# Issuing the spills of decays and convolution results from ScalarE, with two buffers for the decays and one for the results, in a hybrid attention and DeltaNet encoder

## The chip, the cores and the metric

The kernel runs on one core of one Trainium2 chip. The metric is device time in microseconds (us). Before the change three runs gave a median of 2249.93 us (2245.04 to 2252.57).

## The reference, cut to what matters

The program is an encoder of two layers, run on a prompt of 1024 tokens and a sample of 256, 1280 columns in all. Layer 0 is a neighbourhood attention, layer 1 a bidirectional gated DeltaNet with 8 heads, each with keys of 128 and values of 256. The change lies in layer 1:

```python
def _gated_deltanet(h, w_in, conv_w, a_log, dt_bias, norm_w, w_out):
    b, t, _ = h.shape
    proj = h @ w_in
...
    qkv = jax.nn.silu(_centred_depthwise_conv(proj[..., :o1], conv_w))
    z = proj[..., o1:o2].reshape(b, t, GDN_HEADS, GDN_DV)
...
    o_fwd = _chunk_gated_delta(q, k, v, g[:, :, 0], beta[:, :, 0])
    o_bwd = _chunk_gated_delta(fl(q), fl(k), fl(v), fl(g[:, :, 1]), fl(beta[:, :, 1]))
    o = (o_fwd + fl(o_bwd)).astype(h.dtype)
    o = _rmsnorm(o, norm_w) * jax.nn.silu(z)
    return o.reshape(b, t, GDN_VW) @ w_out
```

and in _chunk_gated_delta, for chunks of 64 tokens:

```python
    diff = g[..., :, None] - g[..., None, :]
    decay = jnp.where(tril, jnp.exp(jnp.where(tril, diff, 0.0)), 0.0)
    k_beta = k * beta[..., None]
    a_kk = jnp.where(tril_strict, jnp.einsum('bhncd,bhnsd->bhncs', k_beta, k) * decay, 0.0)
    lhs = jnp.eye(c, dtype=jnp.float32) + a_kk
    w = lax.linalg.triangular_solve(lhs, k_beta * jnp.exp(g)[..., None], left_side=True,
                                    lower=True, unit_diagonal=True)
```

What follows the solve is a scan over the chunks, forward and backward.

## The kernel before

The stages stand one after the other: attention (to about 640 us), its output projection and the norm (to 780), the DeltaNet's projections (gdn_proj, about 780 to 1600), the scan (to about 2040) and the output projection. All five edits lie in gdn_proj, or in what it calls.

**What TensorE does there.** For each head four blocks of 128 output channels are projected (q, k and two of v), then two gate blocks (z). A block takes three passes, wh with xh, wh with xl and wl with xh, for each of 8 slices of the inputs, over column blocks of 512, 512 and 256 (L1250). So TensorE has a stream of matmuls without end, and all else is meant to run beside it. load_w (L1191) brings a block's weights: SyncE loads wraw, ScalarE copies it to wh (L1202) and its negative to wl (L1206), and then a DMA issued by GpSimd adds the weights to wl in flight (L1207), which leaves the rounding error of wh. There are three buffers for wh and wl and one for wraw.

**What runs beside it.** Class Side (L1211) holds chains, Python generators that are stepped by the columns which the matmuls have taken: a chain that yields n is stepped again n times its pace later. The chains are:

- conv (L504): ScalarE makes the middle tap (L509), VectorE the other four (L512), and after a pause ScalarE the Silu into th (L518), which two DMAs spill to DRAM (L519 and L520).
- decays (L614), for one head: six calls of decay (L602). Each is a matmul into a PSUM bank "t" (L605, three buffers), two or four sums on VectorE from it (L608, which end the bank's use), and an exponential in place on ScalarE (L611). E holds two of these and is spilled (L624), and GpSimd adds its halves into B (L625).
- invert (L629), for one head, once its keys have left conv: k by k matmuls, four diagonal blocks turned, and then a sweep of 30 steps on VectorE (L671 and L673) that inverts 32 x 32 blocks. Two transposes (L677 and L678) end the sweep, ScalarE and GpSimd place the results (L686, L687, L692 to L694). Then decays of the next head are put on the side, and after a pause come four groups of small matmuls, L703, L710, L723 and L731, each with copies between them (L706 by ScalarE to Z behind L703; L712 to L718 behind L710; L726 by ScalarE to Z behind L723).
- the gates' z (L554 and L563 with their spills).

**What sets the order.** The program gives the Tile framework the instructions in the order in which these generators run; the framework's scheduler then sets each engine's own order by its model of when each becomes ready. So a changed yield moves what is offered when, and the engine's order follows only as far as the scheduler takes it up. Each engine runs its row in order, a DMA issue too: what stands behind a waiting issue waits with it.

Of the kernel before, what the change touches and what calls it, by code (L numbers as in the profile page):

```python
# [8 lines left out]
F32 = mybir.dt.float32  # L9
# [6 lines left out]
NP, NS = 1024, 256  # L16
T = NP + NS
# [6 lines left out]
def pool(tc, name, bufs, side="left"):  # L24
    return tc.tile_pool(name=name, bufs=bufs, side=side, reuse_waits="tile")
# [436 lines left out]
def gdn_proj(tc, a, pmm, XH, XL):  # L462

    nc = tc.nc
    with ExitStack() as st:
        ap = st.enter_context(pool(tc, "gp", 2, "right"))
        pp = st.enter_context(banks(tc, "gpi", 2, "right"))
        side = a["side"] = Side()
        Bs = {}
# [34 lines left out]
        def conv(f, r):  # L504

            h, ch = divmod(f, 4)
            m = T + 2
            acc = ap.tile([128, T + 2], F32, name="acc")
            nc.scalar.activation(acc, r[:, 2:2 + m], AF.Copy, scale=cw[:, f, 2:3])  # L509
            yield 8000  # L510
            for i in (0, 1, 3, 4):
                tap = nc.vector.scalar_tensor_tensor(acc, r[:, i:i + m], cw[:, f, i:i + 1], acc,  # L512
                                                     op0=OP.mult, op1=OP.add)
                if i == 0:
                    tc.keep_in_program_order(tap)
            yield 14000 if ch == 1 else 20000
            th = ap.tile([128, T + 2], F32, name="th")
            tc.keep_in_program_order(nc.scalar.activation(th, acc, AF.Silu))  # L518
            nc.sync.dma_start(a["qkv_dram"][f, :, :NP], th[:, :NP])  # L519
            nc.sync.dma_start(a["qkv_dram"][f, :, NP:], th[:, NP + 2:])  # L520
            if ch == 1:
                side.add(invert(tc, a, ap, pp, h, th, D, W, WT, Z, Bs), 4000, 0.85 if h == 7 else 0.95)

# [2 lines left out]
        for h, ch in order:  # L526
            f = 4 * h + ch
# [3 lines left out]
            for b in sorted(range(3), key=lambda b: (f, b) not in a["begun"]):  # L531
                t0, n = BLK[b]
# [68 lines left out]

def decay(nc, a, ap, pool, h, d, c0, n, E, nt=2):  # L602

# [3 lines left out]
    for c in range(n):  # L607
        nc.vector.scalar_tensor_tensor(E[:, c], pg[:, 128 * c:128 * c + 128],  # L608
                                       a["lbG"][:, 8 * d + h, c0 + c:c0 + c + 1], a["mask"][:, d],
                                       op0=OP.add, op1=OP.add)  # L610
    nc.scalar.activation(E, E, AF.Exp)  # L611


def decays(tc, a, ap, pp, h, Bs):  # L614

    nc = tc.nc
    B = ap.tile([128, NB, 128], F32, name="B", bufs=2)
    for c0 in range(0, NB, 4):
        n = min(4, NB - c0)
        E = ap.tile([128, 2, 4, 128], F32, name="E", bufs=1)[:, :, :n]  # L620
        for d in range(2):
            decay(nc, a, ap, pp, h, d, c0, n, E[:, d], 3)
            yield 3500
        nc.sync.dma_start(a["e_dram"][h, :, :, c0:c0 + n], E)  # L624
        nc.gpsimd.tensor_add(B[:, c0:c0 + n], E[:, 0], E[:, 1])  # L625
    Bs[h] = B


def invert(tc, a, ap, pp, h, kT, D, W, WT, Z, Bs):  # L629


    nc = tc.nc
# [3 lines left out]
    for c0 in range(0, NB, 4):  # L636
        n = min(4, NB - c0)
# [21 lines left out]
    side, quad = (a["blocks"][:, i, None, :].to_broadcast([128, NB, 128]) for i in range(2))  # L659
# [7 lines left out]
    for c in range(30, 0, -1):  # L667
        tmp = ap.tile([128, 240], F32, name="tmp", bufs=1)
        n = 31 - c
# [24 lines left out]
        nc.gpsimd.tensor_copy(W[sl[i], 1, :, q], diag(i, lo))  # L694
        yield 0
    if h < 7:
        a["side"].add(decays(tc, a, ap, pp, h + 1, Bs), 4000)
    else:
        factors(tc, a)
    yield 34000  # L700
    zt = pp.tile([128, NB, 32], F32, name="m", bufs=2)
    for c in range(NB):
        nc.tensor.matmul(zt[:, c], B32[:, c], M[:, c], start=True, stop=True)  # L703
# [44 lines left out]
def gates(tc, a, ap, pmm, pp, XH, XL):  # L748

    nc = tc.nc  # L750
# [5 lines left out]
    for b in (0, 2, 1):  # L756
        t0, n = BLK[b]
# [39 lines left out]
    eT = consts.tile([128, 16, NB], F32, name="eT")  # L797
    eTG = consts.tile([128, 16, NB], F32, name="eTG")
    pG = pp.tile([128, 16, NB], F32, name="t", bufs=3)
    tri = ap.tile([128, 2, 4, 128], F32, name="E", bufs=1)[:, :, 0]  # L800
    for d, keep in enumerate((OP.is_ge, OP.is_le)):
        nc.vector.tensor_scalar(tri[:, d], a["jp"], 0.0, None, op0=keep)
    for d in range(2):
# [700 lines left out]
```

## Time and profile before

| | us |
|---|---|
| median of three runs | 2249.93 (2245.04 to 2252.57) |
| the profiled execution's own time | 2251.55 |
| its span | 2249.7 |
| TensorE busy, share of the span | 2166.0 (96%) |
| VectorE, ScalarE, GpSimd busy | 1509.2, 1146.6, 585.1 |
| TensorE's clock, mean | 0.98 of full |

All rows of a profile come from the one profiled execution, whose time is 1.6 us over the median. A row of the instructions in order of time has its start, its length, engine, line, operation, out<-in, and in brackets the idle time of the engine ahead of it, with what ended that. Matmuls overlap, so their starts count and not their lengths. A row of waits has the engine and line that waited, on whom, and the total, the times and the longest. A row of stretches has the stretch, and for each engine its busy time in it, and behind them the clock granted to TensorE, the DMA engines' share and GB/s.

### The profile page before, as it was taken

To read this page: it belongs to the slowest core of one execution; us is meant where nothing else is said; L and a number is where in the kernel's file an instruction comes from. 1 tells how busy PE (TensorE), PEld (TensorE's weight loads), DVE (VectorE), ACT (ScalarE), POOL (GpSimd) and SP (SyncE) were. 2 spreads that over 40 slices of the span, in tenths; PEclk is the share of its full clock that TensorE was granted. 3 is DMA by queue.
4 is the path that set the end of the run, shared out by engine and by line. 5 is a ranking of instruction groups with operands and counts; after the bars stand their busy time and mean duration, and the time that the engine had idled before them with its cause. 6 is when DMAs were issued, how large, how long until landed. Compare 5 with 4: busy or idle time off the path is not lost.

```text
span 2249.7 us, 34012 instructions
## 1 busy us (share of the span) xinstructions
PE 2166.0 (96%) x12502; PEld 1881.3 (84%) x12502; DVE 1509.2 (67%) x3370; ACT 1146.6 (51%) x2313; POOL 585.1 (26%) x631
## 2 busy tenths in 40 slices
PE   8999999999999999899999999999899999999998
PEld 7789989989878877788888888888788888877887
DVE  5577777776773858768577676867566666675444
ACT  6455545555673454454544546354456666654333
POOL 2100100110230422233132313231176766600000
PEclk9999999999999999899999999999899999999999
DMA  5424342533556343443534444442675566567322
GB/s 181 112 74 118 82 118 75 125 93 97 151 150 182 98 114 89 141 127 101 159 105 134 111 136 115 128 145 71 209 207 164 168 186 180 154 216 234 107 96 85
DMA packets 148456, 300.10 MB, mean 133 GB/s; under 512 B 44976, under 2 KB 67632, under 8 KB 147264
## 3 DMA queue, kind: packets, MB, share of 16 engines
q1 hardware_dynamic: 126784, 232.89, 32.7%
q0 software_dynamic: 12096, 44.05, 11.2%
q10 hardware_dynamic: 9408, 20.98, 3.0%
q8 instruction: 99, 1.62, 0.3%
q14 instruction: 69, 0.57, 0.1%
HBM read 211.92 MB, written 75.45 MB: 128 GB/s over the span
## 4 chain that ended last, share of the span: by engine, by line
PE 70%; DVE 17%; ACT 5%; DMA 4%; issue 3%; POOL 1%; SPq 0%; ACTq 0%; DVEq 0%; POOLq 0%
PE mm L1250 42%; PE mm L1266 4%; DVE tmp L671 3%; DVE X L673 3%; PE k L1014 3%; PE o L986 2%; PE k L1005 2%; PE O L263 2%; PE o L1027 2%; PE u L986 2%; DVE acc L512 2%; PE pt L243 2%; DMA yt<-y_spill 1%; PE t L940 1%; PE S L286 1%
## 5 line engine op out<-in xcount | busy, mean ns | idle before, releaser
L1250 PE MATMUL mm<-xh,wh 128*128 128x512 f32 (+1 forms) x1920 | 700.6, 365 | 6.3 <-DVE z L554 3.2
L1250 PE MATMUL mm<-xh,wl 128*128 128x512 f32 (+1 forms) x1920 | 700.7, 365 | 3.4 <-DMA wl<-w_o 2.2
L1250 PE MATMUL mm<-xl,wh 128*128 128x512 f32 (+1 forms) x1920 | 701.9, 366 | 0.3 <-DVE xl L352 0.2
L1250 PEld LDWEIGHTS mm<-xh,wh 128*128 128x128 f32 x1920 | 367.6, 191 | 52.8 <-DVE z L554 3.8
L1250 PEld LDWEIGHTS mm<-xh,wl 128*128 128x128 f32 x1920 | 367.5, 191 | 47.6 <-DMA wl<-w_o 2.6
L1250 PEld LDWEIGHTS mm<-xl,wh 128*128 128x128 f32 x1920 | 367.7, 191 | 43.1 <-DVE xl L352 0.4
L512 DVE SCALAR_TENSOR_TENSOR acc<-raw,cw,acc 128x1282 f32<-128x1282 f32 x128 | 199.1, 1555 | 4.7 <-ACT acc L509 2.3
L1202 ACT ACTIVATE wh<-wraw 128x1024 fp32r<-128x1024 f32 x92 | 96.8, 1055 | 139.2 <-PE mm L1250 112.7
L1200 POOL CAST wh<-wraw 128x1024 fp32r<-128x1024 f32 x32 | 34.2, 1070 | 498.2 <-PE mm L1250 441.4
L1250 PE MATMUL mm<-yh,wh 128*128 128x512 f32 (+1 forms) x384 | 137.5, 359 | 2.4 <-ACT yh L1124 2.2
L1250 PE MATMUL mm<-yh,wl 128*128 128x512 f32 (+1 forms) x384 | 137.0, 358 | 1.2 <-DVE wl L1204 1.2
L1250 PE MATMUL mm<-yl,wh 128*128 128x512 f32 (+1 forms) x384 | 137.6, 360 | 0.1
L1018 DVE TENSOR_TENSOR vl<-k,vh 128x256 fp32r<-128x256 f32 x160 | 67.1, 424 | 69.6 <-ACT vh L1017 65.1
L247 ACT ACTIVATE ph<-pt 128x512 fp32r<-128x512 f32 (+2 forms) x144 | 67.6, 479 | 77.0 <-PE pt L243 65.3
L539 ACT ACTIVATE raw<-mm 128x512 f32<-128x512 f32 (+1 forms) x96 | 49.9, 522 | 101.9 <-PE mm L1250 96.1
L248 DVE TENSOR_TENSOR pl<-pt,ph 128x512 fp32r<-128x512 f32 (+2 forms) x144 | 75.2, 538 | 38.2 <-ACT ph L247 36.7
L608 DVE SCALAR_TENSOR_TENSOR E<-t,lbG,mask 128x128 f32<-128x128 f32 x160 | 46.9, 342 | 79.7 <-DMA e_spill<-E 78.8
L1206 ACT ACTIVATE wl<-wraw 128x1024 fp32r<-128x1024 f32 x84 | 88.5, 1053 | 16.3 <-DMA wraw<-w_qk 8.4
L221 ACT ACTIVATE P<-P,mx 128x384 f32<-128x384 f32 (+1 forms) x128 | 75.0, 587 | 39.6 <-DVE mx L220 38.3
L1266 PE MATMUL mm<-wh,xl 128*128 128x256 f32 x320 | 91.9, 287 | 0.6 <-POOL xl L65 0.6
L1017 ACT ACTIVATE vh<-k 128x256 fp32r<-128x256 f32 x160 | 60.6, 380 | 62.5 <-PE k L1014 59.3
L1266 PE MATMUL mm<-wl,xh 128*128 128x256 f32 x320 | 91.6, 286 | 0.5 <-DVE wl L1204 0.5
(314 smaller groups left out, 4917.1 us busy)
## 6 DMA issues: line engine op xcount, KB each, us to landing
wraw<-w_qkv SPq DMA_DIRECT2D x32, 512.0 KB, 3.7
qkv_spill<-th SPq DMA_DIRECT2D x32, 512.0 KB, 2.7
wraw<-w_go SPq DMA_DIRECT2D x32, 512.0 KB, 3.6
wl<-w_qkv POOLq DMA_DIRECT2D x30, 512.0 KB, 8.0
Al<-e_spill SPq DMA_DIRECT2D x8, 1280.0 KB, 6.7
qe<-eg_spill SPq DMA_DIRECT2D x16, 640.0 KB, 8.0
wraw<-w_qk SPq DMA_DIRECT2D x16, 512.0 KB, 3.9
wl<-w_qk POOLq DMA_DIRECT2D x16, 512.0 KB, 8.6
```

The source lines that it names most:

```text
L221: nc.scalar.activation(Pv, Pv, AF.Exp, scale=-1.0, bias=mx[:, 0:1], accum_out=mx[:, 1:2])
L247: nc.scalar.activation(view(ph), view(pt), AF.Copy)
L248: nc.vector.tensor_sub(view(pl), view(pt), view(ph))
L512: tap = nc.vector.scalar_tensor_tensor(acc, r[:, i:i + m], cw[:, f, i:i + 1], acc, op0=OP.mult, op1=OP.add)
L671: nc.vector.tensor_mul(tv, N[:, 0:c, c:c + 1].to_broadcast([128, c, n]), X[:, c:c + 1, c + 1:32].to_broadcast([128, c, n]))
L673: nc.vector.tensor_add(X[:, 0:c, c + 1:32], X[:, 0:c, c + 1:32], tv)
L986: self.tc.nc.tensor.matmul(ps, w[x], v[y], start=(first and i == 0), stop=(i == 2))
L1014: nc.tensor.matmul(pw, W[:, d, cs[d]], Y[d], start=True, stop=True)
L1202: nc.scalar.activation(wh, raw, AF.Copy)
L1206: nc.scalar.activation(wl, raw, AF.Copy, scale=-1.0)
L1250: nc.tensor.matmul(ps, w[:, k, :], x[k][b], start=(k == 0 and i == 0), stop=(k == KD - 1 and i == 2))
L1266: nc.tensor.matmul(ps, x[k][b][:, cc], w[:, k % 4, :], start=(k == 0 and i == 0), stop=(k == KD - 1 and i == 2))
```

## The change

The two DMAs that spill th are issued by ScalarE instead of SyncE, and th has one buffer instead of two. The DMA that spills E is issued by ScalarE as well, and E has two buffers instead of one. The decays of the next head are put on the side with a delay of 12000 columns instead of 4000, and each pause in them is 1.3 times as long. In the first and the last head the pause ahead of L703 is 44000 columns instead of 34000. In gates the tile tri takes the new number of buffers of E, whose name it shares.

```diff
@@ -514,10 +514,10 @@
                 if i == 0:
                     tc.keep_in_program_order(tap)
             yield 14000 if ch == 1 else 20000
-            th = ap.tile([128, T + 2], F32, name="th")
+            th = ap.tile([128, T + 2], F32, name="th", bufs=1)
             tc.keep_in_program_order(nc.scalar.activation(th, acc, AF.Silu))
-            nc.sync.dma_start(a["qkv_dram"][f, :, :NP], th[:, :NP])
-            nc.sync.dma_start(a["qkv_dram"][f, :, NP:], th[:, NP + 2:])
+            nc.scalar.dma_start(a["qkv_dram"][f, :, :NP], th[:, :NP])
+            nc.scalar.dma_start(a["qkv_dram"][f, :, NP:], th[:, NP + 2:])
             if ch == 1:
                 side.add(invert(tc, a, ap, pp, h, th, D, W, WT, Z, Bs), 4000, 0.85 if h == 7 else 0.95)
 
@@ -617,11 +617,11 @@
     B = ap.tile([128, NB, 128], F32, name="B", bufs=2)
     for c0 in range(0, NB, 4):
         n = min(4, NB - c0)
-        E = ap.tile([128, 2, 4, 128], F32, name="E", bufs=1)[:, :, :n]
+        E = ap.tile([128, 2, 4, 128], F32, name="E", bufs=2)[:, :, :n]
         for d in range(2):
             decay(nc, a, ap, pp, h, d, c0, n, E[:, d], 3)
             yield 3500
-        nc.sync.dma_start(a["e_dram"][h, :, :, c0:c0 + n], E)
+        nc.scalar.dma_start(a["e_dram"][h, :, :, c0:c0 + n], E)
         nc.gpsimd.tensor_add(B[:, c0:c0 + n], E[:, 0], E[:, 1])
     Bs[h] = B
 
@@ -694,10 +694,10 @@
         nc.gpsimd.tensor_copy(W[sl[i], 1, :, q], diag(i, lo))
         yield 0
     if h < 7:
-        a["side"].add(decays(tc, a, ap, pp, h + 1, Bs), 4000)
+        a["side"].add(decays(tc, a, ap, pp, h + 1, Bs), 12000, 1.3)
     else:
         factors(tc, a)
-    yield 34000
+    yield 44000 if h in (0, 7) else 34000
     zt = pp.tile([128, NB, 32], F32, name="m", bufs=2)
     for c in range(NB):
         nc.tensor.matmul(zt[:, c], B32[:, c], M[:, c], start=True, stop=True)
@@ -797,7 +797,7 @@
     eT = consts.tile([128, 16, NB], F32, name="eT")
     eTG = consts.tile([128, 16, NB], F32, name="eTG")
     pG = pp.tile([128, 16, NB], F32, name="t", bufs=3)
-    tri = ap.tile([128, 2, 4, 128], F32, name="E", bufs=1)[:, :, 0]
+    tri = ap.tile([128, 2, 4, 128], F32, name="E", bufs=2)[:, :, 0]
     for d, keep in enumerate((OP.is_ge, OP.is_le)):
         nc.vector.tensor_scalar(tri[:, d], a["jp"], 0.0, None, op0=keep)
     for d in range(2):
```

Nothing is computed differently, and each engine has the same instructions but for the 88 DMA issues (32 of L519, 32 of L520, 24 of L624) that ScalarE has and SyncE has no more, and one pair of table loads fewer on ScalarE. What moves is the order.

The first place is on TensorE in one of the middle heads, around the fourth of a head's six decay matmuls (t_12052 before, t_12090 after). mm_12015 is the third column block of one of the head's projections (mm_11999 after), mm_12071 and mm_12047 are the first block of the next. Before:

```order
L1250 MATMUL mm_12015<-xh6_2_7755,wl_11904 128x256
L1250 MATMUL mm_12015<-xh7_2_7758,wh_11903 128x256
L605 MATMUL t_12052<-GR_8791,one_hot_64 128x512 [waits DVE_49,PE_49]
L1250 MATMUL mm_12015<-xl7_2_7782,wh_11903 128x256
L1250 MATMUL mm_12015<-xh7_2_7758,wl_11904 128x256
L1250 MATMUL mm_12071<-xh0_0_7735,wh_12066 128x512 [waits Activation_49]
```

After:

```order
L1250 MATMUL mm_12047<-xh6_0_7753,wh_12042 128x512
L1250 MATMUL mm_12047<-xl6_0_7777,wh_12042 128x512
L1250 MATMUL mm_12047<-xh6_0_7753,wl_12043 128x512
L605 MATMUL t_12090<-GR_8791,one_hot_64 128x512 [waits DVE_49,PE_49]
L1250 MATMUL mm_12047<-xh7_0_7756,wh_12042 128x512
L1250 MATMUL mm_12047<-xl7_0_7780,wh_12042 128x512
L1250 MATMUL mm_12047<-xh7_0_7756,wl_12043 128x512
```

The fourth decay matmul has moved back from the end of one column block to the end of the next; 21 matmuls of 512 columns and 2 of 256 now stand ahead of it that stood behind it.

The second place is on ScalarE in the same head. wraw_12318 holds the weights of the head's first gate block, wh_12320 and wl_12321 are made of it; E_11989 and E_12026 are decays, m_12258 and m_12271 what the matmuls L723 wrote. Before, among the decays:

```order
L539 ACTIVATE raw0_8850<-mm_12015 128x256 [waits PE_49]
L1202 ACTIVATE wh_12320<-wraw_12318 128x1024 [waits DMAHW1_49]
L509 ACTIVATE acc_12062<-raw0_8850,cw_8848 128x1282 [waits Activation_49]
L1206 ACTIVATE wl_12321<-wraw_12318 128x1024 [waits DMASW1_49]
L539 ACTIVATE raw1_8851<-mm_12071 128x512 [waits PE_49]
L611 ACTIVATE E_12026<-E_12026 128x512 [waits DMAHW2_49,DVE_49,Pool_49]
```

After, behind the second group of small matmuls:

```order
L717 ACTIVATE W_8873<-m_12184 32x10x32 [waits DVE_49,PE_49]
L718 ACTIVATE W_8873<-m_12184 32x10x32
L539 ACTIVATE raw0_8850<-mm_12201 128x512 [waits PE_49]
L1202 ACTIVATE wh_12320<-wraw_12318 128x1024 [waits DMAHW1_49]
L726 ACTIVATE Z_8875<-m_12258 64x5x64 [waits PE_49,Pool_49]
L726 ACTIVATE Z_8875<-m_12258 64x5x64
L1206 ACTIVATE wl_12321<-wraw_12318 128x1024 [waits DMASW1_49]
L726 ACTIVATE Z_8875<-m_12271 64x5x64 [waits PE_49]
L726 ACTIVATE Z_8875<-m_12271 64x5x64
```

wh_12320 and wl_12321 have moved from the decays of the head to its L726 copies. The first matmul that reads wl_12321 stands at the same place of TensorE's row in both, with L731's first. The other four middle heads are alike.

The third place is on VectorE in the first head, at the end of the sweep (X_9265) and behind it. acc_9524 is a convolution, t_9618, t_9648 and t_9633 are the first, second and third decay bank of the next head. Before:

```order
L673 TENSOR_TENSOR X_9265<-X_9265,tmp_9537 128x30 [waits DVE_49]
L608 SCALAR_TENSOR_TENSOR E_9632<-t_9633,lbG_8977,mask_8858 128x128 [waits DMAHW0_49,PE_49,Pool_49]
L677 STREAM_TRANSPOSE N_9545<-X_9265 128x32x32 [waits DVE_49]
L678 STREAM_TRANSPOSE D_8872<-X_9265 128x32x32
L512 SCALAR_TENSOR_TENSOR acc_9524<-raw1_8851,cw_8848,acc_9524 128x1282
L608 SCALAR_TENSOR_TENSOR E_9632<-t_9633,lbG_8977,mask_8858 128x128
L512 SCALAR_TENSOR_TENSOR acc_9524<-raw1_8851,cw_8848,acc_9524 128x1282 [waits DVE_49]
L608 SCALAR_TENSOR_TENSOR E_9632<-t_9633,lbG_8977,mask_8858 128x128
L512 SCALAR_TENSOR_TENSOR acc_9524<-raw1_8851,cw_8848,acc_9524 128x1282 [waits DVE_49]
L608 SCALAR_TENSOR_TENSOR E_9632<-t_9633,lbG_8977,mask_8858 128x128
```

After:

```order
L608 SCALAR_TENSOR_TENSOR E_9617<-t_9618,lbG_8977,mask_8858 128x128
L671 TENSOR_TENSOR tmp_9537<-N_9264,X_9265 128x30 [waits DVE_49]
L608 SCALAR_TENSOR_TENSOR E_9617<-t_9618,lbG_8977,mask_8858 128x128
L673 TENSOR_TENSOR X_9265<-X_9265,tmp_9537 128x30 [waits DVE_49]
L677 STREAM_TRANSPOSE N_9545<-X_9265 128x32x32 [waits DVE_49]
L678 STREAM_TRANSPOSE D_8872<-X_9265 128x32x32
L512 SCALAR_TENSOR_TENSOR acc_9524<-raw1_8851,cw_8848,acc_9524 128x1282 [waits Activation_49]
L608 SCALAR_TENSOR_TENSOR E_9617<-t_9648,lbG_8977,mask_8858 128x128 [waits PE_49]
L512 SCALAR_TENSOR_TENSOR acc_9524<-raw1_8851,cw_8848,acc_9524 128x1282 [waits DVE_49]
L608 SCALAR_TENSOR_TENSOR E_9617<-t_9648,lbG_8977,mask_8858 128x128
L512 SCALAR_TENSOR_TENSOR acc_9524<-raw1_8851,cw_8848,acc_9524 128x1282 [waits DVE_49]
L608 SCALAR_TENSOR_TENSOR E_9617<-t_9648,lbG_8977,mask_8858 128x128
```

Before, the sums of the first and second bank were done within the sweep, and those of the third stand among the taps. After, those of the first stand at the sweep's end, and those of the second among the taps. On TensorE the fourth decay matmul of that head now follows 14 matmuls of 512 columns and 16 of 256 later, the fifth 21 of 512 columns behind the fourth, and both still stand ahead of L703. In the last head L703 stands at the same place of TensorE's row within two matmuls.

## The prediction

> **What bounds the kernel now.** I read the page first, its busy times.
>
> ```profile
> PE 2166.0 (96%) x12502; PEld 1881.3 (84%) x12502; DVE 1509.2 (67%) x3370; ACT 1146.6 (51%) x2313; POOL 585.1 (26%) x631
> ```
>
> TensorE is busy for 96% of the span. All five edits lie in the DeltaNet projection stage (about 780 to 1600 us), so they can only win or lose what TensorE idles there, and the slow clock behind each idle time. Second view: TensorE's waits (total, times, longest), of the whole program, then of 960 to 1500 us alone.
>
> ```profile
> PE t L605 <- DVE E L608: 17.0, 6, 3.3
> PE m L703 <- ACT X L686: 4.6, 1, 4.6
> PE m L703 <- issue: 4.1, 1, 4.1
> PE mm L1250 <- DVE z L554: 3.2, 2, 2.6
> PE m L731 <- issue: 1.7, 1, 1.7
> ```
>
> ```profile
> PE t L605 <- DVE E L608: 16.6, 5, 3.3
> ```
>
> Between 960 and 1500 us stand five like stretches, 100 us each; I call them the steady heads. TensorE idles 3.3 us in each, ahead of a decay matmul (L605). The rest of the list lies in the first and the last head. Third view: TensorE and VectorE in order of time in one steady head, and the granted clock in the 10 us after each of the five waits, after the last head's L703 and after the first head's.
>
> ```profile
> 1163.38 0.73 PE L605 MATMUL t<-GR,one_hot 128*128 128x512 f32 x1 [3.31 <-DVE E L608]
> ...
> 1168.15 0.39 PE L1250 MATMUL mm<-xh,wl 128*128 128x512 f32 x1
> 1168.38 0.39 PE L1250 MATMUL mm<-xh,wh 128*128 128x512 f32 x1
> ```
>
> ```profile
> 1156.10 3.17 DVE L512 SCALAR_TENSOR_TENSOR acc<-raw,cw,acc 128x1282 f32<-128x1282 f32 x2
> ...
> 1162.64 1.63 DVE L608 SCALAR_TENSOR_TENSOR E<-t,lbG,mask 128x128 f32<-128x128 f32 x6
> ```
>
> ```profile
> 1063.00:1073.00 10.00, 10.00 (x39) 8.17 (x40) 2.98 (x12) 6.62 (x9) 3.46 (x5) 0.83 0.53 141
> 1163.40:1173.40 10.00, 10.00 (x39) 8.22 (x40) 3.02 (x12) 6.65 (x9) 3.49 (x6) 0.83 0.51 136
> 1263.80:1273.80 10.00, 10.00 (x35) 8.17 (x36) 3.05 (x12) 5.72 (x9) 3.49 (x6) 0.73 0.54 141
> 1365.10:1375.10 10.00, 10.00 (x39) 8.23 (x40) 3.05 (x12) 6.78 (x9) 3.50 (x6) 0.84 0.55 145
> 1465.40:1475.40 10.00, 10.00 (x50) 8.39 (x50) 3.05 (x12) 8.19 (x10) 3.51 (x6) 1.00 0.53 140
> 1558.00:1568.00 10.00, 9.94 (x40) 8.93 (x41) 0.00 (x0) 6.43 (x9) 0.91 (x3) 0.59 0.34 133
> 888.00:898.00 10.00, 10.00 (x36) 8.65 (x37) 3.40 (x7) 2.55 (x6) 4.37 (x6) 0.54 0.00 0
> ```
>
> The fourth decay of a head needs one of three "t" banks; all hold decays, since VectorE is at the conv taps until then and frees the first bank only in its row of 1162.64. At full clock a matmul of 512 columns comes each 0.23 us (the last two rows of TensorE). After the wait the clock is lower: its column (third from the right) gives what that costs, ten times one minus the clock. After the five waits: 1.7, 1.7, 2.7, 1.6 and 0, together 7.7 us; after the last head's wait of 4.10 us: 4.1; after the first head's of 4.57: 4.6. So the steady heads lose 16.6 + 7.7 = 24.3 us, 4.9 each.
>
> **The change part by part.** *Steady heads, what goes.* In the changed order the fourth decay stands behind 23 more matmuls (21 of 512 columns, 2 of 256): 21 by 0.23 and 2 by about half of it, 5.0 us. TensorE came to it at 1163.38 − 3.31 = 1160.07, and so comes at about 1165.1. VectorE now does all four taps first (6.3 us by the row of two) from 1156.1, then the four sums of the first bank (6 in 1.63, so 1.1): free at 1163.5. The wait goes, with 1.6 us to spare. I take off all 24.3 us.
>
> *Steady heads, what comes.* In all five the copy wl (L1206) of the head's first gate block moves from the head's start to behind two copies L726, which read what the matmuls L723 write. Rows of before, on ScalarE, GpSimd and TensorE:
>
> ```profile
> 1194.80 0.88 ACT L726 ACTIVATE Z<-m 64x320 f32<-64x320 f32 x2 [0.18 <-PE m L723]
> ```
>
> ```profile
> 1200.81 0.47 PE L1250 MATMUL mm<-xh,wl 128*128 128x512 f32 x1
> ```
>
> ```profile
> 1118.69 1.05 ACT L1206 ACTIVATE wl<-wraw 128x1024 fp32r<-128x1024 f32 x1
> ```
>
> ```profile
> 1120.03 0.86 POOL L1207 DMA_DIRECT2D wl<-w_qkv  x1 [13.25 <-ACT wl L1206]
> ```
>
> ```profile
> wl<-w_z POOLq DMA_DIRECT2D x11, 512.0 KB, 7.7
> ```
>
> ```profile
> DMA to landing us min/median/max: 5.8/7.9/9.6
> ```
>
> TensorE's matmul of 1200.81 is the first that reads this wl; the matmuls between the L723 that releases the two L726 and this one are the same ones in the new order. So 1200.81 − 1194.80 = 6.0 us are left from the start of those L726 to the use. The new way takes 0.88 (L726) + 1.05 (copy) + 0.29 (1118.69 + 1.05 to 1120.03, copy to DMA issue) + 7.7 (the median landing of gate weights between 960 and 1500 us) = 9.9. TensorE waits 3.9 us. With the landings' ends of 5.8 and 9.6 it waits 2.0 to 5.8; I take 3.9, since 11 gate loads give that median. What hid this load before is gone: it was copied among the decays at the head's start, a long way ahead of its use. Behind a wait of 3.9 us I put the slow clock of the nearest row, the 4.1 us after 4.10 idle; its bounds are 0 (the fifth 3.3-us wait) and 4.6. A head then loses 8.0 us, five 40.0; bounds 2.0 and 10.4 a head.
>
> The Trainium skill, "TensorE: Matmul & The Clock Gate", Part 1, says that the clock halves after one idle window of about 3.4 us and comes back after about 3.4 us of busy array. By it a slow phase costs about 1.7 us, an estimate from that page; four of the five waits of 3.3 us cost about that or more, the 4.1 after 4.10 idle goes against it, and the sum would be some 12 us lower by the page.
>
> *Issue on ScalarE.* 88 issues move (rows: instructions, minimum, median and maximum ns):
>
> ```profile
> L519 SPq DMA_DIRECT2D qkv_spill<-th x32: 319/320/408, 819.6 to 1590.9; - x32
> ...
> L520 SPq DMA_DIRECT2D qkv_spill<-th x32: 423/426/474, 820.0 to 1591.3; - x32
> ...
> L624 SPq DMA_DIRECT2D e_spill<-E x24: 513/525/582, 821.6 to 1484.6; - x24
> ...
>   DVE E L608: 78.8, 13
> ```
>
> At SyncE's durations, 32 × 0.32 + 32 × 0.43 + 24 × 0.53 = 36.4 us of ScalarE, which is idle for 49% of the span: 0 on the path, except where copies for TensorE queue behind. The only near one is L706 ahead of L710: behind it the new order puts L624's issues and the last E; I find ScalarE done about when TensorE comes, so 0, at most 1.5 us a head. SyncE no longer holds up loads behind spills, but TensorE waits for no such load in this stage: 0. The second E buffer removes VectorE's 78.8 us of waits for spills; these are beside TensorE's work: 0 beyond the L605 wait already counted. One buffer for th makes a Silu wait for the spill ahead of it, a full projection earlier: 0.
>
> *First head.* A row of TensorE, then rows of VectorE:
>
> ```profile
> 872.13 0.47 PE L605 MATMUL t<-GR,one_hot 128*128 128x512 f32 x1 [0.44 <-DVE E L608]
> ```
>
> ```profile
> 883.63 1.56 DVE L512 SCALAR_TENSOR_TENSOR acc<-raw,cw,acc 128x1282 f32<-128x1282 f32 x1
> 885.12 0.34 DVE L608 SCALAR_TENSOR_TENSOR E<-t,lbG,mask 128x128 f32<-128x128 f32 x1
> ```
>
> Of the list of waits, this head has the 4.6 at L703, the 1.7 at L731 and the 2.6 at L1250 on z; with the 0.44 above, 9.3 us. Slow clock costs about as much (4.6 behind L703, the rest an estimate at the same rate): 19 in all. In the new order the fourth and fifth decay both stand ahead of L703. The fourth stands 14 matmuls of 512 columns and 16 of 256 later, 5.1 us: it comes at 876.8 (from 872.13 − 0.44) and waits for four sums put at the sweep's end, done about 878.3 by the place of the sweep: 1.5 us. The fifth comes 21 matmuls of 512 columns later, 4.8 us, so at 883.1, and needs a bank whose four sums stand between the four taps behind the sweep's transposes. The sweep now holds five sums fewer (five times 0.27), so the first tap begins at 882.3 and the last sum ends four pairs of 1.76 later (885.12 + 0.27 − 883.63): 889.3, a wait of 6.2. L703 follows without one. With 4.6 of slow clock, and some 2 left of the later waits, 14 us: a gain of 5 (bounds: 8 gained, if the later waits go, 3 lost, if they stay).
>
> *Last head.* 44000 columns for 34000 should move L703, which waited 4.10 us; but the scheduler's new order leaves L703 at its place among the projection's matmuls, only L710 and later stand further back. 0, at most 0.5 lost.
>
> **Sum.** −24.3 + 40.0 − 5 = +10.7 us on the profiled execution's 2251.55. That is 1.6 over the median of the three times, 2249.93, so the forecast is 2249.93 + 10.7 = 2260.6, say 2260. A measurement of this kernel tells about 0.3%, 6.8 us, from no change.
>
> **The rivals.** *The weights land in time to spare the clock* (faster). The mechanism is wl's landing in the steady heads. If the new place has a landing of 5.8 to 7.0 us, TensorE waits 2.0 to 3.2, and short of 3.3 idle the clock need not fall, as after the fifth wait (1.00). The point is a landing of 7.1. At 6.4 the wait is 2.6: 13 − 24.3 − 5 = −16, 2234 us. For it: the row's minimum of 5.8. Against: the median, and that the next raw load starts behind the copy as it always did and shares the DMA engines.
>
> *Short slow phases* (no change). The wait is 3.9, but it costs 1.7 of clock, as three of the five waits of 3.3 us did: 5 × 5.6 = 28.0; 28.0 − 24.3 − 5 = −1.3, 2249 us. For it: these rows; against it: the 4.1 and 4.6 after the two longer ones. It is what the Trainium skill's page on the clock gate, Part 1, gives.
>
> *ScalarE becomes late* (slower still). L706's last copy comes after TensorE stands at L710: 1.5 us and as much slow clock in five heads, +15 on top: 2275. For it: 4.6 us of issues a head (36.4 over 8) put into ScalarE's strict order; against it: 49% idle.
>
> *The change doesn't do what it says*, in one place: the last head, above; there it costs nothing and stands in every case.
>
> **How the numbers follow.** Forecast 0.38, early weights 0.28, short slow phases 0.23, late ScalarE 0.11. Faster by over 0.3% (under 2243.2): 0.28. Within: 0.23. Slower (over 2256.7): 0.49. Range: from early weights, 2232, to past late ScalarE, 2282. The bounds of all terms together would give 2249.9 + 2.0 × 5 − 24.3 − 8 = 2228 and 2249.9 + 10.4 × 5 − 24.3 + 3 + 7.5 = 2288; the range leaves out their joint ends. The forecast's own range, with waits of 3.3 to 4.8 us, is 2257 to 2266.
>
> **What would show it.** Right: no wait of L605 on L608 between 960 and 1500 us; in its place TensorE's L1250 waiting for DMA wl<-w_z five times, 2 to 6 us, each with clock 0.5 behind it; the first head with a wait at L605 in place of L703's; the last head as before. Wrong: no wait for wl<-w_z, or one under 2 us; L605's waits still there; L710 waiting for L706; the slices after the waits at full clock.

## The result and the profile after

The changed kernel takes 2273.49 us (median of four runs, 2273.12 to 2274.58), beside 2247.90 us for the kernel before (four runs, 2245.04 to 2252.57): a ratio of 1.0113, 95% interval 1.0093 to 1.0132, so 21 to 30 us slower. The prediction had 2260 in a range of 2232 to 2282, with slower as the likeliest side. The side was right; the loss is more than twice the 10.7 us that it summed up.

The profiled execution after the change has 2273.12 us and a span of 2271.3, against 2251.55 and 2249.7 before: 21.6 us more. Its busy times from the page:

```profile
PE 2174.8 (96%) x12502; PEld 1889.1 (83%) x12502; DVE 1523.7 (67%) x3370; ACT 1146.1 (50%) x2311; POOL 595.7 (26%) x631
```

As before, TensorE is busy 96% of the span, so this page part says nothing of where 21.6 us came from. TensorE's waits over the whole program do (total, times, longest); the rows left out lie in other stages:

```profile
PE mm L1250 <- DMA wl<-w_z: 15.5, 4, 4.6
PE m L710 <- ACT Z L706: 7.0, 4, 2.7
...
PE m L703 <- issue: 5.3, 1, 5.3
PE mm L1250 <- DVE z L554: 4.8, 4, 1.9
...
PE t L605 <- DVE E L608: 3.9, 1, 3.9
...
PE mm L1250 <- DMA wl<-w_qkv: 3.0, 1, 3.0
```

The 17.0 us of L605 are down to 3.9, and that one wait lies in the first head: in the steady heads none is left. In its place stand late weights wl, one wait in each of the five heads: in four of them those of the first gate block (w_z, 15.5), in the fifth those of a projection block (w_qkv, 3.0), which the order puts at this place there. Then L710 waits for L706 (7.0, four heads), and L1250 for z (3.4 of the 4.8 us). These last two had no share in the forecast. Now TensorE in order of time at one wait of each kind, the first head's L605 first:

```profile
889.32 0.55 PE L605 MATMUL t<-GR,one_hot 128*128 128x256 f32 x1 [3.87 <-DVE E L608]
...
1071.09 3.28 PE L710 MATMUL m<-X,Z 128*128 128x32 f32 x20 [1.44 <-ACT Z L706]
...
1096.41 0.79 PE L1250 MATMUL mm<-xh,wl 128*128 128x512 f32 x1 [4.27 <-DMA wl<-w_z]
```

The granted clock (third column from the right) in the 10 us from each wait, for four L710 and the first, third and fourth wl waits (behind the second, of 2.45 us, it is 1.00, behind the fifth, of 2.97 us, 0.84):

```profile
1071.10:1081.10 10.00, 10.00 (x40) 8.61 (x41) 5.74 (x7) 5.69 (x8) 1.45 (x2) 0.66 0.25 93
1096.40:1106.40 10.00, 9.99 (x39) 8.71 (x40) 2.97 (x4) 0.00 (x0) 1.97 (x2) 0.66 0.14 54
1179.90:1189.90 10.00, 9.96 (x40) 8.46 (x41) 6.33 (x7) 5.65 (x8) 1.50 (x2) 0.66 0.25 93
1283.80:1293.80 10.00, 10.00 (x57) 8.70 (x57) 6.42 (x7) 7.08 (x9) 1.41 (x2) 1.00 0.24 92
1306.20:1316.20 10.00, 9.99 (x42) 8.71 (x43) 3.71 (x4) 0.20 (x1) 1.97 (x2) 0.74 0.21 78
1389.30:1399.30 10.00, 9.96 (x40) 8.73 (x41) 5.74 (x7) 5.72 (x8) 1.50 (x2) 0.66 0.24 93
1414.60:1424.60 10.00, 9.97 (x41) 8.68 (x42) 3.31 (x4) 0.00 (x0) 1.97 (x2) 0.70 0.13 54
```

Three of four L710 waits have 0.66 behind them: 3.4 us lost to the clock each, more than the 1.44 us that TensorE idles in the first two. TensorE's busy column is full in all seven rows; only the clock column shows this loss.

Heads are measured from a head's first L641 to the next one's (the eight starts are 828.8, 917.0, 1013.5, 1113.9, 1214.3, 1315.7, 1415.9 and 1502.2 us before, the stage's end with the first L927 or L940 at 1603.2; after: 829.0, 904.7, 1005.3, 1113.1, 1217.0, 1322.2, 1431.0, 1520.4 and 1625.0). "First" is the first two stretches, "steady" the five in the middle. e1 and e10 are experiments, below:

| us | first | steady (five) | last | all |
|---|---|---|---|---|
| before | 184.7 | 488.7 | 101.0 | 774.4 |
| after | 176.3 | 515.1 | 104.6 | 796.0 |
| after − before | −8.4 | +26.4 | +3.6 | +21.6 |
| forecast | −5 | +15.7 | 0 | +10.7 |
| e1, issue on SyncE again | 173.3 | 462.5 | 104.8 | 740.6 |
| e10, and no 44000 | 172.0 | 462.5 | 104.2 | 738.7 |

The stage accounts for all of the 21.6 us.

### The profile page after: what moved, and what is told of

The parts are those of the page before. It is cut to its first block, busy times and chain, and to the rows that moved or that the text cites. A ratio compares the mean times of both kernels' runs of the same rounds, so it can differ in the third digit from the quotient of the medians.

```text
span 2271.3 us, 33983 instructions
## 1 busy us (share of the span) xinstructions
PE 2174.8 (96%) x12502; PEld 1889.1 (83%) x12502; DVE 1523.7 (67%) x3370; ACT 1146.1 (50%) x2311; POOL 595.7 (26%) x631
## 3 DMA queue, kind: packets, MB, share of 16 engines
q1 hardware_dynamic: 111040, 201.43, 29.1%
## 4 chain that ended last, share of the span: by engine, by line
PE 67%; DVE 16%; DMA 6%; ACT 5%; issue 4%; POOL 1%; ACTq 0%; SPq 0%; DVEq 0%; POOLq 0%
PE mm L1250 40%; DVE acc L512 4%; PE mm L1266 3%; PE k L1014 3%; PE o L986 2%; PE k L1005 2%; DVE tmp L671 2%; PE o L1027 2%; PE u L986 2%; PE O L263 2%; DVE X L673 2%; PE pt L243 2%; DMA wl<-w_z 1%; PE m L710 1%; DMA yt<-y_spill 1%
## 5 line engine op out<-in xcount | busy, mean ns | idle before, releaser
L1250 PE MATMUL mm<-xh,wl 128*128 128x512 f32 (+1 forms) x1920 | 705.0, 367 | 22.7 <-DMA wl<-w_z 15.5
L1250 PE MATMUL mm<-xh,wh 128*128 128x512 f32 (+1 forms) x1920 | 705.0, 367 | 7.8 <-DVE z L554 4.8
L1250 PE MATMUL mm<-xl,wh 128*128 128x512 f32 (+1 forms) x1920 | 704.8, 367 | 0.3 <-DVE xl L352 0.2
L1250 PEld LDWEIGHTS mm<-xh,wl 128*128 128x128 f32 x1920 | 369.5, 192 | 67.4 <-DMA wl<-w_z 16.1
L1250 PEld LDWEIGHTS mm<-xh,wh 128*128 128x128 f32 x1920 | 369.9, 193 | 53.9 <-DVE z L554 5.9
L1250 PEld LDWEIGHTS mm<-xl,wh 128*128 128x128 f32 x1920 | 369.2, 192 | 43.4 <-DVE xl L352 0.4
L512 DVE SCALAR_TENSOR_TENSOR acc<-raw,cw,acc 128x1282 f32<-128x1282 f32 x128 | 210.8, 1647 | 31.1 <-ACT acc L509 28.2
L1250 PE MATMUL mm<-yh,wh 128*128 128x512 f32 (+1 forms) x384 | 137.5, 359 | 1.8 <-ACT yh L1124 1.8
L1250 PE MATMUL mm<-yh,wl 128*128 128x512 f32 (+1 forms) x384 | 137.1, 359 | 1.2 <-DVE wl L1204 1.2
L1250 PE MATMUL mm<-yl,wh 128*128 128x512 f32 (+1 forms) x384 | 137.8, 360 | 0.3 <-DVE yl L1125 0.3
L539 ACT ACTIVATE raw<-mm 128x512 f32<-128x512 f32 (+1 forms) x96 | 49.8, 521 | 105.7 <-PE mm L1250 97.9
L1266 PE MATMUL mm<-wh,xh 128*128 128x256 f32 x320 | 91.8, 288 | 0.0
```

Of the source, the lines that this page charges most:

```text
L1250: nc.tensor.matmul(ps, w[:, k, :], x[k][b], start=(k == 0 and i == 0), stop=(k == KD - 1 and i == 2))
L1266: nc.tensor.matmul(ps, x[k][b][:, cc], w[:, k % 4, :], start=(k == 0 and i == 0), stop=(k == KD - 1 and i == 2))
```

## The experiments

The theory: what is left of the loss is the two waits that the moved spills bring, wl's copy behind L726 and L706 behind an E, while the later decays and the second E buffer are a gain. The rival: the issue's own time on ScalarE, or the later decays themselves, cost it. All kernels compute everything that the kernel before does. Times are medians, ratios those to the kernel before on the same chip, with 95% intervals. Some kernels were measured on different chips, so the stretches of the profiles say where a difference between two of them lies.

**e1: spills issued by SyncE again, all else as changed.**

```diff
-            nc.scalar.dma_start(a["qkv_dram"][f, :, :NP], th[:, :NP])
-            nc.scalar.dma_start(a["qkv_dram"][f, :, NP:], th[:, NP + 2:])
+            nc.sync.dma_start(a["qkv_dram"][f, :, :NP], th[:, :NP])
+            nc.sync.dma_start(a["qkv_dram"][f, :, NP:], th[:, NP + 2:])
...
-        nc.scalar.dma_start(a["e_dram"][h, :, :, c0:c0 + n], E)
+        nc.sync.dma_start(a["e_dram"][h, :, :, c0:c0 + n], E)
```

> The changed kernel with its three spill DMAs issued by SyncE again; all other edits stay. In its order wl of the first gate block is copied early again in all five steady heads, L710 stands interleaved with projection matmuls again, and the fourth decay keeps its late place. Theory (the two new waits of TensorE, on wl and at L710, cost 29 and 17 us of the changed kernel, slow clock included, and both come from ScalarE's row being moved by the issues): 2273.5 - 46 = 2227 us, with no wait on wl<-w_z, none of L710, none of L605 in the steady heads. Rival (the later decays or the buffers cost the time, and the issue on ScalarE is harmless): 2265 to 2275 us.

2215.53 us, 0.9839 [0.9824, 0.9854]. The three moved lines cost the changed kernel some 58 us (2273.49 − 2215.53; in the profiles the stage is 796.0 − 740.6 = 55.4 us shorter, 52.6 of it in the steady heads), and the rest of the change is worth 37 (2252.85 before − 2215.53). In the steady heads no wait of TensorE is left at all. From 820 to 1610 us its list begins so:

```profile
PE m L703 <- issue: 5.1, 1, 5.1
PE t L927 <- ACT q L924: 4.9, 2, 3.3
PE t L605 <- DVE E L608: 4.0, 1, 4.0
```

All three lie in the first and last head or behind it. The granted clock from 1000.5 to 1463 us is 1.00. So 462.5 us is what the five heads take with no wait and no slow clock, and the losses can be counted from there: 26.2 before (24.3 in the prediction), 52.6 after. Why the two waits are gone stands in ScalarE's row, here of e1 (start, length, line, operation):

```profile
1055.54 1.05 ACT L1202 ACTIVATE wh<-wraw 128x1024 fp32r<-128x1024 f32 x1
1056.48 1.05 ACT L1206 ACTIVATE wl<-wraw 128x1024 fp32r<-128x1024 f32 x1
1057.43 1.74 ACT L706 ACTIVATE Z<-m 32x320 f32<-32x320 f32 x4
```

and of the changed kernel in the same head:

```profile
1064.34 0.87 ACT L706 ACTIVATE Z<-m 32x320 f32<-32x320 f32 x2 [0.17 <-ACT raw L539]
1069.29 0.42 ACT L611 ACTIVATE E<-E 128x256 f32<-128x256 f32 x1 [4.08 <-DVE E L608]
1069.72 0.43 ACT L706 ACTIVATE Z<-m 32x320 f32<-32x320 f32 x1
...
1070.61 0.43 ACT L706 ACTIVATE Z<-m 32x320 f32<-32x320 f32 x1
...
1085.94 0.87 ACT L726 ACTIVATE Z<-m 64x320 f32<-64x320 f32 x2 [3.45 <-PE m L723]
1086.84 1.06 ACT L1206 ACTIVATE wl<-wraw 128x1024 fp32r<-128x1024 f32 x1
```

VectorE at the same time:

```profile
1062.12 6.56 DVE L512 SCALAR_TENSOR_TENSOR acc<-raw,cw,acc 128x1282 f32<-128x1282 f32 x3
1068.61 1.11 DVE L608 SCALAR_TENSOR_TENSOR E<-t,lbG,mask 128x128 f32<-128x128 f32 x4
```

In e1 the gate block's two copies come first and the four L706 stand together. After the change, two L706 come, then an E that waits 4.08 us for VectorE, which has three taps ahead of its sums (to 1068.61), and only behind it the third and fourth L706: done at 1071.04, and TensorE goes on at 1071.09. wl's copy stands behind the two L726. In the changed kernel the wl load then goes on GpSimd, with its landing below:

```profile
1088.19 0.87 POOL L1207 DMA_DIRECT2D wl<-w_z  x1 [12.53 <-ACT wl L1206]
```

```profile
DMA to landing us min/median/max: 8.2/8.2/8.2
```

1088.19 + 8.2 = 1096.39, and the waiting matmul starts at 1096.41. Both waits are explained to within 0.05 us.

**e2: decays at the old time.**

```diff
-        a["side"].add(decays(tc, a, ap, pp, h + 1, Bs), 12000, 1.3)
+        a["side"].add(decays(tc, a, ap, pp, h + 1, Bs), 4000)
```

> The changed kernel with the decays' delay and pace as before (4000, 1); all other edits stay. In its order wl is copied early again, the fourth decay is early again (so the L605 wait of 3.3 us a head returns), and L710 stands in one batch behind L706 as in the changed kernel. Theory: +24 for L605's waits, -29 for wl, L710's 17 stay: 2268 us. Rival (L710's wait costs only its idle 7 us, and wl more than I count): 2255 to 2260. Rival (the later decays are what costs): 2250.

2245.87 us, 0.9974 [0.9960, 0.9989]: much less than expected, so that expectation fell. The waits of L605 are back, and the one on wl and the one at L710 are gone. TensorE's waits from 1005 to 1460 us, the L710 of one head, and the clock in the 10 us from it:

```profile
PE t L605 <- DVE E L608: 16.3, 5, 3.3
```

```profile
1077.58 2.32 PE L710 MATMUL m<-X,Z 128*128 128x32 f32 x20
```

```profile
1077.60:1087.60 10.00, 10.00 (x59) 8.73 (x57) 7.47 (x8) 6.12 (x7) 2.04 (x2) 1.00 0.27 99
```

So the new waits need the later decays and the moved spills together: the spills without the later decays make about the old kernel.

**e3: wl of the head's first gate block made on VectorE**, by a subtraction there in place of ScalarE's copy and GpSimd's adding DMA.

```diff
-            for _ in range(n):
+            for j in range(n):
...
-                gate_z(tc, a, pmm, XH, XL, h, side, (i,))
+                gate_z(tc, a, pmm, XH, XL, h, side, (i,), n == 2 and j == 0)
...
-def gate_z(tc, a, pmm, XH, XL, h, side, halves=(0, 1)):
+def gate_z(tc, a, pmm, XH, XL, h, side, halves=(0, 1), dve=False):
...
-    ws = [load_w(tc, a, a["w_z"][2 * h + i]) for i in halves]
+    ws = [load_w(tc, a, a["w_z"][2 * h + i], eng=nc.vector if dve else None) for i in halves]
```

> The changed kernel, but wl of the first gate block of four of the steady heads is made by VectorE from wraw and wh (one subtraction) in place of ScalarE's copy and GpSimd's adding DMA; nothing else moves on TensorE. Theory (the wait is the DMA's landing): the four waits on wl<-w_z, 15.5 us, and the slow clock behind them, about 9 us, go: 2249 us; L710's waits and the last head's wl wait stay. Rival (what is late is ScalarE as a whole, so wh or another copy takes the place of wl): 2265 to 2273.

2249.74 us, 0.9988 [0.9977, 1.0000], as expected: some 24 us less than the changed kernel. The four waits on the gate blocks' wl go, and the steady heads take 490.8 us instead of 515.1, 24.3 less; the edit reaches a gate block of the first head too (at 847 us), and the first two stretches take 181.9 us instead of 176.3. The waits of L710 and on z stay (1005 to 1460 us):

```profile
PE m L710 <- ACT Z L706: 5.7, 4, 1.4
PE mm L1250 <- DVE z L554: 3.3, 4, 1.3
```

The clock from the second and third L710:

```profile
1171.50:1181.50 10.00, 9.99 (x40) 8.53 (x41) 5.11 (x6) 5.67 (x8) 1.47 (x2) 0.66 0.25 93
1272.20:1282.20 10.00, 10.00 (x47) 8.47 (x48) 5.31 (x7) 7.08 (x9) 1.41 (x2) 0.83 0.24 92
```

All five L710 have a clock of 0.66 or 0.83 behind them.

**e4: L710 later.**

```diff
-    yield 8000
+    yield 12000
     w = pp.tile([128, NB, 32], F32, name="m", bufs=2)
```

> The changed kernel with the pause ahead of L710 at 12000 columns instead of 8000. In its order L710 comes about 1.3 us later, mostly interleaved with projection matmuls, and wl of the first gate block is copied early again. Theory: both new waits go, the later decays keep L605 free: 2227 us, up to 2235 if L710 still waits a few tenths in each head. Rival (the waits pass on to L723 and L731, which stand closer behind L710 now): 2250 to 2265.

2243.40 us, 0.9957 [0.9941, 0.9974]: 30 less than the changed kernel, 16 more than expected. Both waits leave, but others come (1005 to 1460 us), and ScalarE shows the cause of one:

```profile
PE mm L1250 <- DVE z L554: 10.2, 5, 3.5
PE t L641 <- ACT th L518: 4.6, 3, 3.4
PE m L710 <- ACT Z L706: 0.9, 3, 0.3
```

```profile
1103.63 1.06 ACT L1202 ACTIVATE wh<-wraw 128x1024 fp32r<-128x1024 f32 x1 [8.18 <-DMA wraw<-w_qkv]
1104.60 1.26 ACT L518 ACTIVATE th<-acc 128x1282 f32<-128x1282 f32 x1
```

The raw load for that wh stands on SyncE behind the spill of W (L734, issued at 1093.73 after 14.2 us of waiting for VectorE's L733), and the Silu that TensorE waits for stands on ScalarE behind wh. Here a wait that was pushed back came out at the next instruction of a row that is in order.

**e5: e1 with the two conv spills on ScalarE. e6: e1 with the decay spill on ScalarE.** The issue's own time by itself, 64 and 24 issues.

```diff
 e5, against e1
-            nc.sync.dma_start(a["qkv_dram"][f, :, :NP], th[:, :NP])
-            nc.sync.dma_start(a["qkv_dram"][f, :, NP:], th[:, NP + 2:])
+            nc.scalar.dma_start(a["qkv_dram"][f, :, :NP], th[:, :NP])
+            nc.scalar.dma_start(a["qkv_dram"][f, :, NP:], th[:, NP + 2:])
 e6, against e1
-        nc.sync.dma_start(a["e_dram"][h, :, :, c0:c0 + n], E)
+        nc.scalar.dma_start(a["e_dram"][h, :, :, c0:c0 + n], E)
```

> The kernel of e1 (spills on SyncE, other edits in place; 2215.5 us) with the convolutions' two spill DMAs issued by ScalarE again, 64 of the 88 issues; the decays' stay on SyncE. In its order the steady heads keep wl early and L710 interleaved. Theory (the cost is where wl's copy and L710 come to stand, not the issue's time on ScalarE): 2215 to 2225 us. Rival (ScalarE pays for the issues in time, or holds copies behind a waiting issue): 64/88 of the 58 us that e1 saved come back, about 2258.

> The kernel of e1 with the decays' spill DMA alone issued by ScalarE again, 24 issues. In its order the steady heads keep wl early and L710 interleaved. Theory: 2215 to 2225 us. Rival (issues on ScalarE cost by their number): 24/88 of 58 us, about 2231; rival (it is the decays' issue, ahead of L706 in ScalarE's row, that makes L710 wait): 17 us more, about 2232, with L710 waiting for L706.

2219.06, 0.9848 [0.9828, 0.9869], and 2221.97, 0.9867 [0.9843, 0.9892]. Against e1 these intervals overlap. In both the four steady heads that are whole take 95.3 to 95.4 us, the same as in e1. The rival of issue time falls for the parts: each is free there, and what the medians have over e1's, 3.5 and 6.4 us, lies in the profiles in the first two stretches (178.6 and 182.5 us, 173.3 in e1). Only all together do they give an order of ScalarE's row that has the two waits. No run has all 88 on ScalarE with the order of e1, so for the whole of them this is inferred from the parts.

**e7: the later decays alone, on the kernel before. e12: the buffers alone, on the kernel before.**

```diff
 e7, against before
-        a["side"].add(decays(tc, a, ap, pp, h + 1, Bs), 4000)
+        a["side"].add(decays(tc, a, ap, pp, h + 1, Bs), 12000, 1.3)
 e12, against before
-            th = ap.tile([128, T + 2], F32, name="th")
+            th = ap.tile([128, T + 2], F32, name="th", bufs=1)
...
-        E = ap.tile([128, 2, 4, 128], F32, name="E", bufs=1)[:, :, :n]
+        E = ap.tile([128, 2, 4, 128], F32, name="E", bufs=2)[:, :, :n]
...
-    tri = ap.tile([128, 2, 4, 128], F32, name="E", bufs=1)[:, :, 0]
+    tri = ap.tile([128, 2, 4, 128], F32, name="E", bufs=2)[:, :, 0]
```

> The kernel before with the decays' delay and pace alone (12000, 1.3); all spills on SyncE, one E buffer, two th buffers, 34000 everywhere. Theory (the later decays alone take L605's wait away): 24 us less in the steady heads, 2225 to 2230 us, the first and last head about as before. Rival (with one E buffer the sums wait for the spill, which waits in SyncE's row behind the convolutions', so L605 waits again): 2240 to 2250, with VectorE's waits on e_spill above 79 us and L605 waiting in every head.

> The kernel before with two E buffers and one th buffer alone; spills on SyncE, decays at 4000. In its order the fourth decay matmul stays early. Theory (VectorE's 79 us of waits for e_spill go, but they lie beside TensorE's work; L605 still waits 3.3 us a head): steady heads of 100 us, 2240 to 2250 us. Rival (the sums come earlier without those waits and free the banks): steady heads of 95 to 97 us, 2225.

e7: 2233.93 us, 0.9921 [0.9902, 0.9940], between its theory and its rival. e12: 2242.63, 0.9959 [0.9943, 0.9976], as its theory had it. TensorE's waits from 960 to 1490 us, first of e7, then of e12:

```profile
PE t L605 <- DVE E L608: 3.4, 5, 1.2
```

```profile
PE t L605 <- DVE E L608: 16.4, 5, 3.3
```

The later decays take the L605 waits from 3.3 us to about 0.7 each; the second buffer leaves them. What is left in e7 is VectorE still waiting for E's spills (50.0 us in all; 78.8 before); with the buffer too, e1 has 4.2 left. Of the buffers' own gain some 4 us lie in the first head, whose two stretches are 80.5 and 99.9 us in e12, 88.2 and 96.5 before. Alone the two parts win 17.6 and 8.4 us, together (e10) 38.6. More than half of the 12.6 us more lie in the first head: its two stretches take 184.7 us before, 183.9 in e7, 180.4 in e12 and 172.0 in e10.

**e8: the last head's pause at 68000, on e1.**

```diff
-    yield 44000 if h in (0, 7) else 34000
+    yield 44000 if h == 0 else 68000 if h == 7 else 34000
```

> The kernel of e1 with the pause ahead of L703 in the last head at 68000 columns instead of 44000 (the first head keeps 44000). In its order L703 of the last head now comes about 5.6 us of matmuls later and is interleaved. Theory: the 5.1 us wait of L703 and the 3.9 us of slow clock behind it go: 2206 us. Rival (L723 and L731, now close to the end of the projections, wait in its place): 2212 to 2220.

2218.69 us, 0.9849 [0.9830, 0.9868]: nothing against e1. L703's wait goes, and another takes its place. TensorE, then ScalarE:

```profile
1529.86 0.64 PE L710 MATMUL m<-X,Z 128*128 128x32 f32 x2 [4.41 <-ACT Z L706]
```

```profile
1526.90 1.27 ACT L518 ACTIVATE th<-acc 128x1282 f32<-128x1282 f32 x1 [4.91 <-DMA qkv_spill<-th]
1528.08 1.73 ACT L706 ACTIVATE Z<-m 32x320 f32<-32x320 f32 x4
```

L706 stands behind a Silu that waits for th's single buffer to be spilled. The prediction put that buffer at nothing, and in the changed kernel no Silu waits for a spill; here it is what holds L706 back.

**e9: L710 spread among the projection's matmuls, on the changed kernel**, by holding both in the order in which they are written (PIN[0] is tc.keep_in_program_order). Meant to tell the batch of 20 small matmuls from the wait ahead of it.

```diff
-        nc.tensor.matmul(w[:, c], Z[:, c], M[:, NB + c], start=True, stop=True)
+        PIN[0](nc.tensor.matmul(w[:, c], Z[:, c], M[:, NB + c], start=True, stop=True))
...
-            nc.tensor.matmul(ps, w[:, k, :], x[k][b], start=(k == 0 and i == 0), stop=(k == KD - 1 and i == 2))
+            PIN[0](nc.tensor.matmul(ps, w[:, k, :], x[k][b], start=(k == 0 and i == 0), stop=(k == KD - 1 and i == 2)))
```

> The changed kernel (spills on ScalarE) with the projections' matmuls and L710 held in the program's order, so that the ten L710 stand one by one between projection matmuls instead of in one batch, and about 1 us of matmuls earlier; wl of the first gate block is copied earlier in this order as well (slack for it 8.3 us against a landing of 7.7). L710 has to wait for L706 as in the changed kernel, some 2 to 2.7 us in four or five heads. Theory (a wait of 1.4 us lowers the clock because the batch of ten 32-column matmuls behind it counts as little work): with the batch gone the clock stays at 1.00 behind these waits, steady heads of 97.5 to 98.5 us, 2235 us. Rival (the wait alone lowers it): clock 0.66 to 0.83 in the 10 us behind most of them, heads of 100 to 102 us, 2250 us.

2281.04 us, 1.0131 [1.0116, 1.0146]: a miss. Spread out, L710 comes sooner, its wait for L706 grows to 3.0 to 4.5 us, and the clock behind it is about half:

```profile
PE m L710 <- ACT Z L706: 16.7, 5, 4.5
```

```profile
1073.70:1083.70 10.00, 9.99 (x36) 8.74 (x37) 3.02 (x5) 5.65 (x7) 1.47 (x2) 0.54 0.25 93
```

So for waits of 1.4 us batch and wait were not told apart; waits of 3.0 us and more lower the clock without the batch.

**e10: 34000 in every head, on e1. e11: the first head's decays at the old time, on e1.**

```diff
 e10, against e1
-    yield 44000 if h in (0, 7) else 34000
+    yield 34000
 e11, against e1
-        a["side"].add(decays(tc, a, ap, pp, h + 1, Bs), 12000, 1.3)
+        a["side"].add(decays(tc, a, ap, pp, h + 1, Bs), *((12000, 1.3) if h else (4000, 1)))
```

> The kernel of e1 (2215.5 us) with 34000 columns ahead of L703 in the first and last head too. Theory (the longer pause does little: e1's first head gains from the later decays and the buffers): 2214 to 2220 us. Rival (the pause is what shortens the first head from 88 to 77 us): first head near 88, 2226.

> The kernel of e1 with the decays put on the side in the first head at 4000 columns and pace 1, as before, and 12000 and 1.3 in the others. In its order all six decay matmuls of the first head are out before the sweep ends. Theory (the first head's 4.0 us wait of L605 and the 2.7 us of slow clock behind it go): 2209 us. Rival (L703 waits there instead, as in the kernel before): 2215 to 2222.

e10: 2212.39 us, 0.9822 [0.9808, 0.9837], the fastest kernel here; against e1 (0.9839) within the intervals, so the longer pause does nothing that can be measured. e11: 2219.82, 0.9848 [0.9828, 0.9868]. The first head's L605 wait of 4.0 goes, and L710's comes (820 to 1005 us):

```profile
PE m L710 <- ACT Z L706: 4.4, 2, 2.5
```

## Why the prediction was right in its side and short in its size

- **L605's waits go, −24.3.** Right. None is left in the steady heads, and their loss before, counted over e1's 462.5, is 26.2. e7 and e12 show that the later decays do most of it (3.4 us of L605 left) and the buffers alone none of it; in e1, with both, nothing is left.
- **wl's load comes late, +40.0.** Mechanism and place right, in all five heads; only in the fifth the late block is one of the projection (w_qkv) and not, as the prediction and the text ahead of it have it, the gate block. The idle time was right too: 18.5 us in five waits, 3.7 each (forecast 3.9). The clock term was too big: after four of them 3.4, 0, 2.6 and 3.0 us are lost, and 1.6 after the fifth (which falls into the last head's stretch): 10.6, not 20.5. All together 29.1. e3 removes the four of the gate blocks, 15.5 + 9.0 = 24.5 us, and its steady heads win 24.3. So the row of 4.1 us lost after 4.10 idle was the wrong one to take; the short slow phases of the rival (1.7 each) were nearer. That row of before stands ahead of 20 matmuls of 32 columns in one batch, the wl waits ahead of matmuls of 512 columns with L731's of 64 between them; whether this made the difference was not tried:

```profile
1558.06 4.45 PE L703 MATMUL m<-X,B 128*128 128x32 f32 x20 [4.10 <-issue]
```

- **L710, "0, at most 1.5 us a head".** This is the step that failed, a term put at nothing, and the rival that ScalarE becomes late held instead, in four heads of five, though not for its reason, the time of the issues. The wait kept within the bound of 1.5 us in three heads (1.44) and passed it in one (2.66), but the sum took 0 and no slow clock for it; the mistake was to hold that "ScalarE [is] done about when TensorE comes". I had followed L624's issues and an E to L706, but not that this E waits for a sum behind three taps on VectorE: ScalarE idles 4.08 us in front of it. Not the 0.53 us of an issue, but a wait inherited from another engine. Measured 7.0 idle and 3 × 3.4 slow: 17.2 us where the sum had 0 and the rival 15.
- **z, not in the sum.** L1250 waits for L554's z in three steady heads, 3.4 us, with 1.7 us of slow clock behind one: 5.1. In e3 and e4 these waits stand too (3.3 and 10.2), in e1 not. What moves them was not tried by itself.
- **Steady heads, added up.** 18.5 + 9.0 (the 10.6 without the fifth) + 17.2 + 5.1 = 49.8 of 52.6; 2.8 us are in no wait that I counted. With 26.2 gone this makes the +26.4 of the table, where the forecast had +15.7.
- **Issue on ScalarE, 0.** Right as far as its own time goes in the steady heads (e5, e6). The cost, 58 us, is the order that it brings: e1 undoes just these lines.
- **First head, −5.** −8.4. The wait at L605 that was to take L703's place came, 3.9 us for the forecast's 6.2, with 2.8 of slow clock (0.72 over 10 us) for 4.6. That 4.6 was itself read too low: its row begins at 888.0, and the waiting matmul at 886.92; from 886.9 the clock is 0.50 over 10 us, 5.0 us.
- **Last head, 0.** +3.6: L703 waits 5.26 for 4.10 us (clock 0.55 for 0.59, 0.4 more), L723 0.8, and the fifth wl wait's 1.6 of slow clock. This account is not whole, since in e1 and e10, which lack that wl wait, the last head is 3.8 and 3.2 us longer too. As forecast, 44000 columns do not move L703, and e10 loses nothing without them.

So the sum missed by two terms of opposite sign: wl 11 us too high, L710 and z 22 too low. Of the causes, wl and the order of ScalarE's row were shown by taking them away (e1, e3, e5, e6); that L710's slow clock comes with its wait was argued from comparison.

## What to carry to other kernels

An instruction that is moved to another engine costs its place in that engine's order more than its own time: look, for each copy that the busiest engine reads, at what the instructions now ahead of it wait for, on every engine. Where a scheduler decides the order, try the parts of a change one at a time: here the later decays won 17.6 us and the buffers 8.4, both together 38.6, and the moved issues turned that into a loss of 21 to 30. And price a wait with the slow clock behind it, as a range: for waits of 1.4 to 4.6 us it ran from nothing to 5.0 us.

## What was not expected of the hardware

A short wait can cost more in clock than in idle time. Behind L710's waits of 1.4 to 2.7 us the clock over 10 us was 0.66 in three heads of four after the change, and 0.66 or 0.83 in five of five in e3. The Trainium skill, "TensorE: Matmul & The Clock Gate", Part 1, puts the halving after one idle window of about 3.4 us; these waits are shorter and go against it. The same 20 small matmuls without a wait ahead of them left the clock at 1.00 (e2, all five heads), and so did a wait about as long ahead of matmuls of 512 columns. That wait, in the changed kernel's first head, and the clock behind it:

```profile
926.72 0.50 PE L1250 MATMUL mm<-xh,wh 128*128 128x512 f32 x1 [1.46 <-DVE z L554]
```

```profile
926.70:936.70 10.00, 8.58 (x37) 6.81 (x38) 9.49 (x32) 3.40 (x6) 1.50 (x2) 1.00 0.88 274
```

At 1.4 us this points to the two together, but no run had the one changed and the other not: e9 was meant to and did not. With a slightly longer wait the batch is not needed. This one, in the changed kernel, stands between projection matmuls alone, and the clock behind it is 0.83:

```profile
1450.93 0.50 PE L1250 MATMUL mm<-xh,wh 128*128 128x512 f32 x1 [1.88 <-DVE z L554]
```

```profile
1450.90:1460.90 10.00, 9.96 (x37) 8.07 (x38) 9.28 (x26) 1.93 (x3) 0.88 (x1) 0.83 0.61 163
```

In e11 a wait of 1.94 us ahead of an L710 that is spread among projection matmuls has 0.66 behind it. So what the rival of early weights leaned on, that short of 3.3 us idle the clock need not fall, does not hold for every wait.

Nor does one length of wait have one price. wl waits of 4.27, 4.60 and 4.20 us lost 3.4, 2.6 and 3.0 us to the clock, the last head's L703 wait before, 4.10 us, lost 4.1. The wl wait of 2.45 us lost nothing, and neither did one of 1.87 us on z in e12's first head, where the one of 1.88 us above lost 1.7.
